# A hybrid state-space, attention and expert block: a new layout of the state-space powers, a shorter phase doubling, a moved norm, and four diagonals on another engine

## Chip, cores and metric

The kernel runs on one core of one Trainium2 chip. The metric is the device time of one execution in microseconds, taken as the median of several runs. The engines are named as the profile names them: PE (TensorE, matmuls; PEld its weight loads), DVE (VectorE), ACT (ScalarE), POOL (GpSimd), and SP, whose queue starts most DMA transfers.

## The reference

The input is 512 tokens of width 1024 in fp32, a memory of 256 tokens, and stream positions. One layer computes, cut to what matters here:

```python
h = rms(x); z = h @ w_in                 # columns: u_ssm 512, c_q 768, c_kv 256, k_rope 32
# (A) state-space: 32 groups of 16 channels, 64 complex states each
a_bar = exp(lam * dt); b_bar = ((a_bar - 1) / lam) * b
states = scan(s_t = a_bar * s_{t-1} + b_bar @ u_t); y = Re(c @ states) + d * u
y = gelu(y); y_ssm = y * sigmoid(y @ w_glu + b_glu)
# (B) latent attention, 8 heads
q = rms(c_q, q_norm_g) @ w_q_up; kv = rms(c_kv, kv_norm_g) @ w_kv_up; rotary; chunk mask
x = x + concat(rms(y_ssm), rms(y_mla)) @ w_out
x = x + cross_attention(rms(x), rms(mem, norm_mem_g))     # 4 heads, 256 memory tokens
x = x + experts(rms(x))                                   # top-1 of 4 groups, top-2 of 8 experts
return rms(x)
```

## The kernel before, in words

Dense weights are used in two parts, a high part `hi` rounded to a shorter float and the rest `lo`, and each product is three matmuls (`mm3`, lines 264 to 269: hi x hi, hi x lo, lo x hi). `next_w` (189) delivers the next weight tile: SP loads `raw`, ACT makes `hi` (204) and DVE subtracts to get `lo` (214). Three `raw`, three `hi` and three `lo` buffers rotate. Activations are split in the same way by `split` (271 to 278), the high part on ACT and the low part on DVE.

The order of the work in the front of the program:
- The input is transposed and split without its norm; the square sums give the row factor `rx` (416), POOL's `pow` being used for the root (`rstd`, 315). `rx_row` (421) spreads `rx` over columns: four diagonal matrices `dg` are multiplied with ones on PE into `pRX`, and ACT copies that to `RX` (427).
- `s5_params` (463) prepares the state-space part on 128 partitions: powers 0 to 8 of `a_bar` as `are` and `aim` (501 to 517), laid out as [power, group], and the matrices `bs`, `bw`, `cx`, `cy`.
- The first projection makes `u_ssm` (741 to 750; `zq` is scaled with `RX` on DVE), then the keys' and values' latents `pkv` (795 to 803), then the queries' latents `pcq` in six parts (860 to 872). `pz`, `pkv`, `pcq` and `pq` share four PSUM banks in turn; the latents `pkv` are read out by ACT (811) and by DVE's `rope` (789 to 792), and the first `pcq` takes the bank of the first `pkv`.
- The queries' norm follows (874 to 879): a column sum on PE, DVE's copy `sc` (355), POOL's `second_rstd`, and two small DVE products `crq`, `srq`.
- The memory is normed and transposed by `norm_T` (331 to 345, called at 889): for each of two tiles a square sum on ACT (329), scale and root on POOL (317, 318), scaling on ACT (338); then for each of eight column blocks two transposes on PE into one of two PSUM banks and a split into `mT` on ACT and DVE.
- The queries are formed (`pq`, 898 to 912), and the memory's values (`pxv`, 955 to 972).

The state-space part runs beside these. A plan by steps (102, 751 to 764) says after which weight tile each piece is put in: `s5_phase` (577) at step 3, and for each quarter q of the groups `s5_a` (619), `s5_b` (656), `s5_d` (686), `s5_e` (722). A piece is queued behind the last weight or matmul instructions issued by then (`aside`, 174). `s5_a` builds `G` (635 to 637) and `V` (648 to 650) on DVE; the operand `vk` of `V` takes the eight powers as innermost index:

```python
def vk(a):
    return a[:, 1:9, gs].rearrange("p k g -> p g k")[:, :, None, :].to_broadcast([128, 8, 16, 8])
```

`s5_phase` squares a unit phase eight times, renormalising each time, with eight DVE operations per level on 16 elements (591 to 598), and then builds the table `tb` by doubling (606 to 613).

After this front come the attention, the output projection, the cross-attention and the experts. The experts' weights (`gu`, `dn`) are loaded by SP into the buffers that the stages before set free (217 on), and the order on each engine is otherwise set by a list with priorities when the program is built.

Of the kernel before, what the change touches and what calls it, by code (L numbers as in the profile page):

```python
# [15 lines left out]
AF = mybir.ActivationFunctionType  # L16
OP = mybir.AluOpType
# [4 lines left out]
NT = 4  # L22
# [82 lines left out]
def build(tc, I, out, dbg=None, stop=None):  # L105
    nc = tc.nc
# [132 lines left out]
    for i in range(8):  # L239
# [4 lines left out]
        n, k = divmod(i, 4)  # L244
# [53 lines left out]
    ident = C.tile([128, 128], F32, name="ident")  # L298
# [29 lines left out]

        return nc.scalar.activation(spare, src, AF.Square, accum_out=acc)

    def norm_T(tiles, name, n_tok, dst, spare, srcs=None):

        st = C.tile([128, 2, 4], F32, name=f"st_{name}")
        for t, a in enumerate(tiles):
          with hp_(HN):
            square_sum(st[:, 0, t:t + 1], a, spare(t))
            rstd(st[:, 1, t:t + 1], st[:, 0, t:t + 1], 1, D)
            nc.scalar.activation(srcs[t] if srcs else a, a, AF.Copy, scale=st[:, 1, t:t + 1])
        src = srcs or tiles
        for k in range(8):  # L340
            ps = bankt(f"pT_{name}{k}")
            for t in range(len(tiles)):
                nc.tensor.transpose(ps[:, t * 128:(t + 1) * 128], src[t][:, k * 128:(k + 1) * 128], ident)
            hi, lo = dst(k)
            split(hi, lo, ps[:, :n_tok], gain(name, k))
# [38 lines left out]
    rx, rx2 = x_st[:, 1], x_st[:, 2]  # L384
    w0 = next_w("ssm")
    rx, rx2 = x_st[:, 1], x_st[:, 2]
# [34 lines left out]
    def rx_row():  # L421
        ps = bankt("pRX")
        for t in range(NT):
            dg = M.tile([128, 128], F32, name=f"dg{t}", tag="sq")
            nc.gpsimd.tensor_scalar(dg, ident, rx[:, t:t + 1], 1.0, OP.mult, OP.mult)
            nc.tensor.matmul(ps[:, t * 128:t * 128 + 128], ones1.to_broadcast([128, 128]), dg, start=True, stop=True)
        nc.scalar.activation(RX, ps, AF.Copy)

# [34 lines left out]
    def s5_params():  # L463
# [3 lines left out]
        def t(name, shape, dt=F32, tag=""):  # L467
            p[name] = SP.tile(shape, dt, name=f"s5_{name}", tag=tag or f"s5_{name}")
            return p[name]
# [37 lines left out]
        for n in (1, 2, 4):  # L507
# [8 lines left out]
            v.tensor_tensor(aim[:, o], are[:, i], bi, OP.mult)  # L516
            v.tensor_tensor(aim[:, o], aim[:, o], t1, OP.add)

        am, den, fre, fim, t0 = (t(n, [128, 32]) for n in ("am", "den", "fre", "fim", "t0"))
        v.tensor_scalar(am, are[:, 7], -1.0, None, OP.add)  # L520
        v.tensor_tensor(den, lre, lre, OP.mult)
# [55 lines left out]
    def s5_phase(p):  # L577
        v = nc.vector

        def t(name, shape, dt=F32, tag=""):  # L580
            return SP.tile(shape, dt, name=f"s5_{name}", tag=tag or f"s5_{name}")

        ph = p["ph"]

        t2 = t("t2", [128, 4, 16])
        pw = t("pw", [128, 6, 2, 16])
        cur = ph
        for lvl in range(-2, 6):
            nx = pw[:, lvl] if lvl >= 0 else t(f"ph{lvl}", [128, 2, 16])
            c0, s0 = cur[:, 0], cur[:, 1]  # L590
            v.tensor_tensor(t2[:, 0], c0, c0, OP.mult)
            v.tensor_tensor(t2[:, 1], s0, s0, OP.mult)
            v.tensor_tensor(t2[:, 2], t2[:, 0], t2[:, 1], OP.add)  # L593
            v.tensor_scalar(t2[:, 2], t2[:, 2], -1.0, 2.0, OP.mult, OP.add)
            v.tensor_tensor(t2[:, 0], t2[:, 0], t2[:, 1], OP.subtract)
            v.scalar_tensor_tensor(t2[:, 3], c0, 2.0, s0, OP.mult, OP.mult)
            v.tensor_tensor(nx[:, 0], t2[:, 0], t2[:, 2], OP.mult)
            v.tensor_tensor(nx[:, 1], t2[:, 3], t2[:, 2], OP.mult)
            cur = nx

        tb = p["tb"] = u("KV", [128, 2, 16, 64], F32, "s5tb")
        tt = t("tt", [128, 2, 16, 32], tag="s5gt")
        nc.gpsimd.memset(tb[:, 0, :, 0:1], 1.0)
        nc.gpsimd.memset(tb[:, 1, :, 0:1], 0.0)
        pl_ = nc.gpsimd if TP else v
        for lvl in range(6):
            n = 1 << lvl
            c_, s_ = (pw[:, lvl, a, None, :, None].to_broadcast([128, 2, 16, n]) for a in range(2))
            o = tb[:, :, :, n:2 * n]
            pl_.tensor_tensor(tt[:, :, :, 0:n], tb[:, :, :, 0:n], s_, OP.mult)  # L610
            pl_.tensor_tensor(o, tb[:, :, :, 0:n], c_, OP.mult)
            pl_.tensor_tensor(o[:, 0], o[:, 0], tt[:, 1, :, 0:n], OP.subtract)
            pl_.tensor_tensor(o[:, 1], o[:, 1], tt[:, 0, :, 0:n], OP.add)
# [5 lines left out]
    def s5_a(p, q):  # L619

        gs = slice(8 * q, 8 * q + 8)
        v = nc.vector
        pg_ = nc.gpsimd if GP & 1 else v
        ph_ = nc.gpsimd if GP & 2 else v

        g_ = SP.tile([128, 8, 9, 16], F32, name=f"s5G{q}", tag="s5G", bufs=2)
        gt = SP.tile([128, 8, 9, 16], F32, name=f"s5gt{q}", tag="s5gt")

        def ck(a):
            return a[:, :, gs].rearrange("p k g -> p g k")[:, :, :, None].to_broadcast([128, 8, 9, 16])  # L630

        def cm(a):
            return a[:, gs, None, :].to_broadcast([128, 8, 9, 16])

        pg_.tensor_tensor(g_, ck(p["are"]), cm(p["cx"]), OP.mult)
        pg_.tensor_tensor(gt, ck(p["aim"]), cm(p["cy"]), OP.mult)
        pg_.tensor_tensor(g_, g_, gt, OP.add)

        vs = SP.tile([128, 8, 16, 8], F32, name=f"s5vs{q}", tag="s5vs")
        vt = SP.tile([128, 8, 16, 8], F32, name=f"s5vt{q}", tag="s5gt")  # L640

        def vk(a):
            return a[:, 1:9, gs].rearrange("p k g -> p g k")[:, :, None, :].to_broadcast([128, 8, 16, 8])

        def vm(a):
            return a[:, gs, 0:16, None].to_broadcast([128, 8, 16, 8])

        ph_.tensor_tensor(vs, vk(p["are"]), vm(p["bs"]), OP.mult)
        ph_.tensor_tensor(vt, vk(p["aim"]), vm(p["bw"]), OP.mult)
        ph_.tensor_tensor(vs, vs, vt, OP.add)  # L650
        rc = SP.tile([128, 4, 64], F32, name=f"s5rc{q}", tag="s5rc", bufs=2)
        nc.scalar.activation(rc, p["rp"][:, 4 * q:4 * q + 4, None].to_broadcast([128, 4, 64]), AF.Copy)
        nc.gpsimd.memset(rc[:, :, 0:1], 0.0)
        return dict(G=g_, vs=vs, rc=rc)
# [216 lines left out]
            nc.vector.tensor_tensor(sqa, sqa, sq, OP.add)  # L871
        step()
    rq = C.tile([128, NT], F32, name="rq")
    colsum_rstd(rq, sqa, 768, "q", True)
    nc.gpsimd.tensor_scalar(rq, rq, 96.0 ** -0.5, 1.0, OP.mult, OP.mult)
    crq, srq = C.tile([128, NT, 16], F32, name="crq"), C.tile([128, NT, 16], F32, name="srq")
    rqb = rq[:, :, None].to_broadcast([128, NT, 16])
    nc.vector.tensor_tensor(crq, cos, rqb, OP.mult)
    nc.vector.tensor_tensor(srq, sin, rqb, OP.mult)

    mT = [u("H", [128, 4, 2, 256], F32R, f"mT{i}") for i in range(2)]

# [3 lines left out]
    def mv(k, c0=0, c1=256):  # L886
        return mT[k // 4][:, k % 4, 0, c0:c1], mT[k // 4][:, k % 4, 1, c0:c1]

    norm_T([mm_t[:, t] for t in range(2)], "norm_mem_g", 256, m_dst,
           lambda t: mT[0][:, 2 * t:2 * t + 2].rearrange("p k a t -> p (k a t)"))  # L890


    Q = [u("H", [128, 2, 8, 100], F32, f"Q{i}") for i in range(2)]
# [1085 lines left out]
```

## Time and profile before

| | |
|---|---|
| median of 3 runs | 732.78 us (732.72 to 732.96) |
| the profiled execution | 733.54 us |
| its span, first to last instruction | 731.4 us |
| busy: PE, DVE, ACT, POOL | 682.5 us, 416.3 us, 248.7 us, 113.8 us |
| mean granted clock of PE | 0.978 |
| DMA moved | 165.84 MB |

The span is what the trace shows; the profiled execution's own time is 2.1 us longer, and 0.76 us longer than the median. A busy share over the whole span averages stages that are limited by different things, so the views below are cut to stretches. In a wait, the engine and line behind the arrow are what came last by the trace. The granted clock is the share of TensorE's full speed.

### The profile page before, as it was taken

What the parts mean: (1) busy time and instruction counts of PE and PEld (TensorE: products, weight loads), DVE (VectorE), ACT (ScalarE), POOL (GpSimd) and SP (SyncE); (2) the same over time, 40 slices, a digit from 0 to 9 for tenths busy, and PEclk for the clock granted to TensorE, in tenths of its full rate; (3) what the DMA queues carried; (4) which work ended last, traced back from release to release, by engine and by line L of the source; (5) the groups of instructions that cost most, each with busy time, mean ns of one, the idle gap of its engine ahead of it and who ended that gap; (6) DMA issues with size and microseconds to landing.
All of it is one profiled execution on the core that took longest, in us unless ns stands there. A gap on an engine that the chain in (4) does not pass through costs nothing.

```text
span 731.4 us, 10262 instructions
## 1 busy us (share of the span) xinstructions
PE 682.5 (93%) x3684; PEld 469.9 (64%) x3684; DVE 416.3 (57%) x975; ACT 248.7 (34%) x511; POOL 113.8 (16%) x172
## 2 busy tenths in 40 slices
PE   5998988987999999999999999999998999998875
PEld 4696877975878887888878788963333333433333
DVE  4799997957477887555466543552533421221127
ACT  5642354344565766334345422221101000000023
POOL 6300002003300001102000001212332232232100
PEclk9999999999999999999999999999999999999996
DMA  7773132435452254232328896869999999999983
GB/s 213 168 206 109 38 74 67 114 123 127 145 164 68 92 153 131 99 84 84 107 80 339 271 338 240 282 251 390 409 408 408 410 404 410 407 413 388 397 337 121
DMA packets 102013, 165.84 MB, mean 227 GB/s; under 512 B 32762, under 2 KB 64606, under 8 KB 98120
## 3 DMA queue, kind: packets, MB, share of 16 engines
q1 hardware_dynamic: 95512, 157.58, 61.0%
q0 software_dynamic: 6432, 7.58, 3.1%
q8 instruction: 30, 0.49, 0.3%
q14 instruction: 23, 0.19, 0.1%
q10 hardware_dynamic: 16, 0.00, 0.0%
HBM read 154.59 MB, written 25.69 MB: 246 GB/s over the span
## 4 chain that ended last, share of the span: by engine, by line
PE 52%; DMA 28%; DVE 13%; ACT 2%; issue 2%; SPq 1%; POOL 0%; DVEq 0%; ACTq 0%
DMA gu<-moe_w_up 15%; DMA dn<-moe_w_down 6%; PE pG L1784 3%; DVE lo L214 2%; PE po L1034 2%; DMA raw<-w_in 2%; PE pX L1443 2%; PE pxq L268 2%; PE pxq L266 2%; PE pxq L267 2%; DMA gu<-moe_w_gate 2%; PE pD L1841 2%; PE pxo L266 2%; PE pPT L1023 2%; PE pxo L267 2%
## 5 line engine op out<-in xcount | busy, mean ns | idle before, releaser
L1784 PE MATMUL pG<-gu,XT 128*64 128x512 f32 x512 | 126.7, 595 | 5.3 <-DMA gu<-moe_w_up 5.2
L214 DVE TENSOR_TENSOR lo<-raw,hi 128x1024 fp32r<-128x1024 f32 (+3 forms) x64 | 75.9, 1190 | 60.5 <-ACT hi L204 60.1
L204 ACT ACTIVATE hi<-raw 128x1024 fp32r<-128x1024 f32 (+3 forms) x64 | 63.9, 1002 | 102.0 <-issue 21.1
L1784 PEld LDWEIGHTS pG<-gu,XT 128*64 128x64 f32 x512 | 40.4, 136 | 71.8 <-issue 68.5
L1841 PE MATMUL pD<-dn,aT 128*64 128x512 f32 x256 | 73.2, 601 | 1.8 <-DMA dn<-moe_w_down 1.8
L1807 DVE SCALAR_TENSOR_TENSOR a<-pG,RS,sl 128x256 f32<-128x256 f32 x16 | 10.7, 670 | 105.8 <-ACT sl L1801 65.4
L1801 ACT ACTIVATE sl<-pG,RS 128x256 f32<-128x256 f32 x16 | 7.6, 474 | 131.9 <-PE pG L1784 131.9
L1841 PEld LDWEIGHTS pD<-dn,aT 128*64 128x64 f32 x256 | 20.5, 136 | 36.4 <-issue 31.6
L1417 DVE TENSOR_TENSOR XT<-pX,gmo 128x512 f32<-128x512 f32 x32 | 22.0, 686 | 20.9 <-PE pX L1768 16.8
L1803 POOL TENSOR_SCALAR YY<-XG,F 128x1024 f32<-128x1024 f32 x13 | 15.2, 1169 | 107.1 <-issue 46.9
L1768 PEld LDWEIGHTS pX<-ident,XG 128*128 128x128 f32 x120 | 15.7, 194 | 25.0 <-issue 17.2
L1849 DVE SCALAR_TENSOR_TENSOR YY<-pD,GT,YY 128x512 f32<-128x512 f32 x26 | 19.5, 749 | 21.1 <-PE pD L1841 21.0
L1827 ACT ACTIVATE aT<-pA 128x256 f32<-128x256 f32 x16 | 6.1, 384 | 61.4 <-PE pD L1841 46.0
L1768 PE MATMUL pX<-ident,XG 128*128 128x128 f32 x120 | 21.0, 298 | 5.3 <-DMA XG<-hd,IX 5.2
L267 PE MATMUL pxq<-gT,hi 128*128 128x512 f32 x64 | 25.6, 400 | 0.0
L266 PE MATMUL pxq<-gT,hi 128*128 128x512 f32 x64 | 25.5, 399 | 0.0
L268 PE MATMUL pxq<-gT,lo 128*128 128x512 f32 x64 | 25.4, 396 | 0.0
L266 PE MATMUL pcq<-hT,hi 128*128 128x512 f32 x48 | 20.0, 416 | 2.8 <-DVE s_t L593 2.8
L267 PE MATMUL pq<-lo,cq 128*128 128x384 f32 x48 | 18.1, 376 | 2.3 <-DVE lo L214 2.3
L268 PE MATMUL pcq<-hT,lo 128*128 128x512 f32 x48 | 19.7, 410 | 0.0
L267 PE MATMUL pcq<-hT,hi 128*128 128x512 f32 x48 | 19.5, 407 | 0.0
L1855 POOL DMA_INDIRECT xd<-YY,IY x14 | 14.7, 1047 | 30.7 <-DVE YY L1849 25.7
(617 smaller groups left out, 1690.0 us busy)
## 6 DMA issues: line engine op xcount, KB each, us to landing
gu<-moe_w_gate SPq DMA_DIRECT2D x64, 512.0 KB
gu<-moe_w_up SPq DMA_DIRECT2D x64, 512.0 KB
dn<-moe_w_down SPq DMA_DIRECT2D x30, 1024.0 KB
raw<-w_in SPq DMA_DIRECT2D x9, 512.0 KB
raw<-xattn_w_v SPq DMA_DIRECT2D x8, 512.0 KB
raw<-xattn_w_k SPq DMA_DIRECT2D x8, 512.0 KB
raw<-w_out SPq DMA_DIRECT2D x8, 512.0 KB
raw<-xattn_w_q SPq DMA_DIRECT2D x8, 512.0 KB
```

Of the source, the lines that this page charges most:

```text
L204: anchor["act"] = nc.scalar.activation(hi, r, AF.Copy)
L214: anchor["dve"] = nc.vector.tensor_tensor(lo, r, hi.bitcast(F32), OP.subtract)
L266: i = nc.tensor.matmul(o, lh, rh, start=start, stop=False)
L267: nc.tensor.matmul(o, lh, rl, start=False, stop=False)
L268: anchor["pe"] = nc.tensor.matmul(o, ll, rh, start=False, stop=stop)
L1417: return v.tensor_tensor(xt, ps.rearrange("p (k t) -> p k t", k=4), gmo[:, 4 * c:4 * c + 4, None].to_broadcast([128, 4, 128]), OP.mult)
L1768: i = nc.tensor.transpose(ps[:, k * 128:k * 128 + 128], xg[:, 4 * c + k], ident)
L1784: i = nc.tensor.matmul(pg[64 * s:64 * s + 64], xt[c][:, kk, 64 * s:64 * s + 64], ew[2 * n + s, c][:, :, kk], start=k == 0, stop=k == 7)
L1803: nc.gpsimd.tensor_scalar(result(n), XG[n % 2], F1[:, n:n + 1], 1.0, OP.mult, OP.mult)
L1841: i = nc.tensor.matmul(pd[64 * s:64 * s + 64], at_[:, f, 64 * s:64 * s + 64], ew[2 * n + s, 2][:, f, c * 512:c * 512 + 512], start=f == 0, ...
L1849: yield v.scalar_tensor_tensor(o, pd, GT[:, n:n + 1], o, OP.mult, OP.add)
L1855: nc.gpsimd.indirect_dma_start(out=o, out_offset=bass.IndirectOffsetOnAxis(ap=IY[:, w, n:n + 1], axis=0), in_=Y, in_offset=None, bounds_ch ...
```

## The change

Four edits:
- In `s5_params` two ACT copies write `ake`, the powers 1 to 8 of `are` and `aim` as [group, power]. In `s5_a` the operand `vk` reads `ake`, whose eight powers lie side by side.
- In `s5_phase` a level has five DVE operations: both squares in one, the renormalising factor with its sign turned, the difference and the double product with their signs turned, and one product of both with the factor.
- `norm_T` takes a function `mid`, called between its norms and its transposes. The queries' norm becomes that function for the memory, so it is issued behind the memory's norms and ahead of its transposes.
- The four diagonals `dg` are made by ACT (a copy with a scale) and not by POOL.

```diff
--- before.py
+++ after.py
@@ -328,7 +328,7 @@
 
         return nc.scalar.activation(spare, src, AF.Square, accum_out=acc)
 
-    def norm_T(tiles, name, n_tok, dst, spare, srcs=None):
+    def norm_T(tiles, name, n_tok, dst, spare, srcs=None, mid=None):
 
         st = C.tile([128, 2, 4], F32, name=f"st_{name}")
         for t, a in enumerate(tiles):
@@ -337,6 +337,8 @@
             rstd(st[:, 1, t:t + 1], st[:, 0, t:t + 1], 1, D)
             nc.scalar.activation(srcs[t] if srcs else a, a, AF.Copy, scale=st[:, 1, t:t + 1])
         src = srcs or tiles
+        if mid is not None:
+            mid()
         for k in range(8):
             ps = bankt(f"pT_{name}{k}")
             for t in range(len(tiles)):
@@ -422,7 +424,7 @@
         ps = bankt("pRX")
         for t in range(NT):
             dg = M.tile([128, 128], F32, name=f"dg{t}", tag="sq")
-            nc.gpsimd.tensor_scalar(dg, ident, rx[:, t:t + 1], 1.0, OP.mult, OP.mult)
+            nc.scalar.activation(dg, ident, AF.Copy, scale=rx[:, t:t + 1])
             nc.tensor.matmul(ps[:, t * 128:t * 128 + 128], ones1.to_broadcast([128, 128]), dg, start=True, stop=True)
         nc.scalar.activation(RX, ps, AF.Copy)
 
@@ -516,6 +518,10 @@
             v.tensor_tensor(aim[:, o], are[:, i], bi, OP.mult)
             v.tensor_tensor(aim[:, o], aim[:, o], t1, OP.add)
 
+        ake = t("ake", [128, 2, 32, 8])
+        for i, a in enumerate((are, aim)):
+            nc.scalar.activation(ake[:, i], a[:, 1:9].rearrange("p k g -> p g k"), AF.Copy)
+
         am, den, fre, fim, t0 = (t(n, [128, 32]) for n in ("am", "den", "fre", "fim", "t0"))
         v.tensor_scalar(am, are[:, 7], -1.0, None, OP.add)
         v.tensor_tensor(den, lre, lre, OP.mult)
@@ -582,20 +588,17 @@
 
         ph = p["ph"]
 
-        t2 = t("t2", [128, 4, 16])
+        t2 = t("t2", [128, 5, 16])
         pw = t("pw", [128, 6, 2, 16])
         cur = ph
         for lvl in range(-2, 6):
             nx = pw[:, lvl] if lvl >= 0 else t(f"ph{lvl}", [128, 2, 16])
-            c0, s0 = cur[:, 0], cur[:, 1]
-            v.tensor_tensor(t2[:, 0], c0, c0, OP.mult)
-            v.tensor_tensor(t2[:, 1], s0, s0, OP.mult)
-            v.tensor_tensor(t2[:, 2], t2[:, 0], t2[:, 1], OP.add)
-            v.tensor_scalar(t2[:, 2], t2[:, 2], -1.0, 2.0, OP.mult, OP.add)
-            v.tensor_tensor(t2[:, 0], t2[:, 0], t2[:, 1], OP.subtract)
-            v.scalar_tensor_tensor(t2[:, 3], c0, 2.0, s0, OP.mult, OP.mult)
-            v.tensor_tensor(nx[:, 0], t2[:, 0], t2[:, 2], OP.mult)
-            v.tensor_tensor(nx[:, 1], t2[:, 3], t2[:, 2], OP.mult)
+
+            v.tensor_tensor(t2[:, 0:2], cur, cur, OP.mult)
+            v.scalar_tensor_tensor(t2[:, 4], t2[:, 0], -2.0, t2[:, 1], OP.add, OP.add)
+            v.tensor_tensor(t2[:, 2], t2[:, 1], t2[:, 0], OP.subtract)
+            v.scalar_tensor_tensor(t2[:, 3], cur[:, 0], -2.0, cur[:, 1], OP.mult, OP.mult)
+            v.tensor_tensor(nx, t2[:, 2:4], t2[:, 4:5].to_broadcast([128, 2, 16]), OP.mult)
             cur = nx
 
         tb = p["tb"] = u("KV", [128, 2, 16, 64], F32, "s5tb")
@@ -639,14 +642,14 @@
         vs = SP.tile([128, 8, 16, 8], F32, name=f"s5vs{q}", tag="s5vs")
         vt = SP.tile([128, 8, 16, 8], F32, name=f"s5vt{q}", tag="s5gt")
 
-        def vk(a):
-            return a[:, 1:9, gs].rearrange("p k g -> p g k")[:, :, None, :].to_broadcast([128, 8, 16, 8])
+        def vk(i):
+            return p["ake"][:, i, gs, None, :].to_broadcast([128, 8, 16, 8])
 
         def vm(a):
             return a[:, gs, 0:16, None].to_broadcast([128, 8, 16, 8])
 
-        ph_.tensor_tensor(vs, vk(p["are"]), vm(p["bs"]), OP.mult)
-        ph_.tensor_tensor(vt, vk(p["aim"]), vm(p["bw"]), OP.mult)
+        ph_.tensor_tensor(vs, vk(0), vm(p["bs"]), OP.mult)
+        ph_.tensor_tensor(vt, vk(1), vm(p["bw"]), OP.mult)
         ph_.tensor_tensor(vs, vs, vt, OP.add)
         rc = SP.tile([128, 4, 64], F32, name=f"s5rc{q}", tag="s5rc", bufs=2)
         nc.scalar.activation(rc, p["rp"][:, 4 * q:4 * q + 4, None].to_broadcast([128, 4, 64]), AF.Copy)
@@ -871,12 +874,14 @@
             nc.vector.tensor_tensor(sqa, sqa, sq, OP.add)
         step()
     rq = C.tile([128, NT], F32, name="rq")
-    colsum_rstd(rq, sqa, 768, "q", True)
-    nc.gpsimd.tensor_scalar(rq, rq, 96.0 ** -0.5, 1.0, OP.mult, OP.mult)
     crq, srq = C.tile([128, NT, 16], F32, name="crq"), C.tile([128, NT, 16], F32, name="srq")
-    rqb = rq[:, :, None].to_broadcast([128, NT, 16])
-    nc.vector.tensor_tensor(crq, cos, rqb, OP.mult)
-    nc.vector.tensor_tensor(srq, sin, rqb, OP.mult)
+
+    def q_norm():
+        colsum_rstd(rq, sqa, 768, "q", True)
+        nc.gpsimd.tensor_scalar(rq, rq, 96.0 ** -0.5, 1.0, OP.mult, OP.mult)
+        rqb = rq[:, :, None].to_broadcast([128, NT, 16])
+        nc.vector.tensor_tensor(crq, cos, rqb, OP.mult)
+        nc.vector.tensor_tensor(srq, sin, rqb, OP.mult)
 
     mT = [u("H", [128, 4, 2, 256], F32R, f"mT{i}") for i in range(2)]
 
@@ -887,7 +892,7 @@
         return mT[k // 4][:, k % 4, 0, c0:c1], mT[k // 4][:, k % 4, 1, c0:c1]
 
     norm_T([mm_t[:, t] for t in range(2)], "norm_mem_g", 256, m_dst,
-           lambda t: mT[0][:, 2 * t:2 * t + 2].rearrange("p k a t -> p (k a t)"))
+           lambda t: mT[0][:, 2 * t:2 * t + 2].rearrange("p k a t -> p (k a t)"), mid=q_norm)
 
 
     Q = [u("H", [128, 2, 8, 100], F32, f"Q{i}") for i in range(2)]
```

## Rows read from the trace of the kernel before

**Rows 1.** The page: busy tenths of the span in 40 equal slices, by engine.

```profile
PE   5998988987999999999999999999998999998875
...
DVE  4799997957477887555466543552533421221127
```

**Rows 2.** Windows: start:end, length, busy time (instructions) by engine, granted clock, DMA, GB/s.

```profile
30.00:156.00 126.00, 115.60 (x715) 99.20 (x714) 115.50 (x282) 52.00 (x96) 6.10 (x26) 0.95 0.40 113
200.00:400.00 200.00, 198.39 (x1158) 162.27 (x1157) 132.78 (x270) 105.39 (x219) 9.11 (x19) 0.99 0.39 124
530.00:700.00 170.00, 157.74 (x709) 60.23 (x708) 47.62 (x105) 10.44 (x27) 47.36 (x46) 1.00 1.01 401
```

**Rows 3.** Waits of PE, 20 to 200 us: total us, times, longest.

```profile
PE pxv L267 <- DVE lo L214: 3.3, 2, 2.1
PE pcq L266 <- DVE s_t L593: 2.8, 1, 2.8
PE pq L267 <- DVE lo L214: 2.3, 1, 2.3
PE pT_norm_mem_g L343 <- ACT mem L338: 2.2, 1, 2.2
...
PE pRX L426 <- POOL dg L425: 1.7, 1, 1.7
```

**Rows 4.** Windows, as Rows 2, right behind the waits at 54.8 and 103 us.

```profile
57.50:60.30 2.80, 2.71 (x7) 2.17 (x8) 2.80 (x20) 0.00 (x0) 0.00 (x0) 0.50 0.60 168
106.00:108.00 2.00, 2.00 (x8) 2.00 (x7) 2.00 (x3) 0.60 (x1) 0.00 (x0) 0.50 0.34 74
```

**Rows 5.** Lines on DVE, 30 to 156 us: count, busy, mean ns, idle before.

```profile
L648 DVE TENSOR_TENSOR s5vs<-s_are,s_bs 128x1024 f32<-128x1024 f32 x4 | 8.2, 2044 | 0.6 <-PE s5vT L680 0.6
L649 DVE TENSOR_TENSOR s5vt<-s_aim,s_bw 128x1024 f32<-128x1024 f32 x4 | 8.0, 2009 | 0.0
...
L635 DVE TENSOR_TENSOR s5G<-s_are,s_cx 128x1152 f32<-128x1152 f32 x4 | 5.4, 1354 | 0.0
...
L650 DVE TENSOR_TENSOR s5vs<-s5vs,s5vt 128x1024 f32<-128x1024 f32 x4 | 5.0, 1238 | 0.0
...
L277 DVE SCALAR_TENSOR_TENSOR mT<-pT_norm_mem_g,G,mT 128x256 fp32r<-128x256 f32 x8 | 3.7, 481 | 3.4 <-ACT mT L276 3.3
```

**Rows 6.** Timeline of DVE around 55 us: start, us, engine, line, tiles.

```profile
53.88 0.20 DVE L591 TENSOR_TENSOR s_t<-s_ph 128x16 f32<-128x16 f32 x1
...
54.83 0.17 DVE L592 TENSOR_TENSOR s_t<-s_ph-2_757 128x16 f32<-128x16 f32 x1
...
56.02 1.22 DVE L214 TENSOR_TENSOR lo<-raw,hi 128x1024 fp32r<-128x1024 f32 x1
...
57.26 0.18 DVE L790 TENSOR_TENSOR rp1k<-pkv,srx 128x32 f32<-128x32 f32 x1
```

**Rows 7.** Timeline of DVE around 103 us.

```profile
100.71 2.01 DVE L648 TENSOR_TENSOR s5vs<-s_are,s_bs 128x1024 f32<-128x1024 f32 x1 [0.62 <-PE s5vT L680]
...
104.47 0.95 DVE L214 TENSOR_TENSOR lo<-raw,hi 128x768 fp32r<-128x768 f32 x1
```

**Rows 8.** Timeline of ACT and POOL: the memory's square sum, then POOL's queue.

```profile
100.28 1.06 ACT L329 ACTIVATE mT<-mem 128x1024 fp32r<-128x1024 f32 x1
...
114.41 0.64 POOL L435 TENSOR_TENSOR rv<-sc,st_x 128x4 f32<-128x4 f32 x1 [28.22 <-DVE sc L355]
...
116.92 1.24 POOL L318 TENSOR_TENSOR st_norm_mem_g<-rv,mhalf 128x1 f32<-128x1 f32 x2
```

**Rows 9.** Timeline of DVE at 151 us.

```profile
151.09 2.35 DVE L214 TENSOR_TENSOR lo<-raw,hi 128x1024 fp32r<-128x1024 f32 x2
```

**Rows 10.** Timeline of POOL and ACT: diagonals, and small ACT operations.

```profile
26.20 0.76 POOL L425 TENSOR_SCALAR dg<-ident,st_x 128x128 f32<-128x128 f32 x2
...
34.06 0.24 ACT L455 ACTIVATE sin<-sck_rope 128x64 f32<-128x64 f32 x1
...
34.36 0.40 ACT L652 ACTIVATE s5rc<-s_rp 128x256 f32<-128x256 f32 x1
```

## The prediction, made before the change was timed

> **What bounds the kernel now.** I read first the page's tenths [rows 1]: PE is full in most slices, and DVE is at 9 in several slices between 20 and 160 us and falls off behind them. Second, the windows [rows 2]. From 30 to 156 us, the stage of all four edits but one, PE is busy 115.6 of 126 us and DVE 115.5, so two engines in strict order share one stage at 92% each. From 200 to 400 us PE is busy 99%, and from 530 to 700 us the DMA queues are full (1.01) and feed the experts' weights. None of the edits touches these two stretches. The weights' loads start as buffers of the dense stages come free, so an earlier front moves PE's stretch and the DMA's stretch forward together. I count a gain in the front one to one.
>
> Third, PE's waits up to 200 us [rows 3]. Four single waits of over 2 us lie in the DVE stage: 2.8 (start of the query latents, `pcq`), 2.3 (`pq`, for a weight's low half), 2.2 (the memory's transposes, for ACT's scaling) and 2.1 (`pxv`, for a low half). That is 9.4 us. One of 1.7 for the diagonals lies ahead of them. [...] At full clock the same cycles take some 0.05 x 126 = 6.3 us less.
>
> **The change part by part.**
>
> *The multiplies of V (L648, L649).* Eight instructions of 1024 elements take 2.04 and 2.01 us on average, 16.2 us together [rows 5]. L650, as large and with all operands in a row, takes 1.24. The old operand steps 32 elements from one power to the next; the new one has the eight powers side by side. L635 also reads a repeated operand and yet takes 1.35 us for 1152 elements, the rate of L650, so repetition alone is not what costs. I take 1.24 us and save 8 x 0.79 = 6.3 us of DVE. The bounds are 1.24, where nothing of the stride is left, and 2.04, where it wasn't the stride. [...]
>
> *Two copies on ACT (`ake`).* 256 elements each; the nearest row is `s5rc`, 128x256 in 0.40 us [rows 10], so 0.8 us. ACT is busy 52 of 126 us [rows 2]. The copies go ahead of the small copies that DVE's `bb` waits for; I charge 0.3 us, between 0 and 0.8.
>
> *Phase doubling.* Eight levels lose three operations each. One level alone takes 0.95 us from start to start (53.88 to 54.83) [rows 6], 0.12 per operation of eight. Five operations, of which three follow each other at about 0.17 to 0.20, give 0.6. Where other work fills the gaps only the issue slot of some 0.09 us is saved (53.88 to 56.02 holds 19 operations and their gaps in 2.14 us). I take 24 x 0.09 = 2.2 us on DVE. The bounds are 8 x 0.1 = 0.8 (all five operations one after another at 0.17, 0.85 instead of 0.95) and 8 x 0.5 = 4.0 (five slots of 0.09 and no gap).
>
> *Diagonals on ACT.* POOL makes two in 0.76 us [rows 10]. On ACT, between 0.24 for 64 elements and 0.40 for 256 [rows 10], one of 128 elements should take some 0.29, and ACT need not stand behind POOL's square of `rx`. The gain on the way to `RX` is 0.4 us, with bounds 1.0 (all four POOL operations against all four of ACT, and no step of POOL before) and a loss of 1.1, one large ACT operation like the 1.06 us one [rows 8] put ahead of them.
>
> *Memory norm ahead of the queries' norm.* No work is added. The second half of the memory's square sum runs on ACT at 100.28, but POOL's queue holds the queries' norm in front, which starts at 114.41 when DVE delivers its sum, and so the memory's root comes at 116.92 [rows 8]. Now POOL can go at 101.4: at most 1.9 us for scale and root (0.64 and 1.24 [rows 8]), then two scalings of about 1.1 us on ACT (the size of the 1.06 row) end near 105.5, some 11 us before the root stands today. The whole wait of 2.2 goes. Moved back in turn is the queries' norm with `crq` and `srq`; its POOL queue is rid of the memory's operations, and the queries' evacuation needs it only when the first `pq` tiles are summed, so I cost it at nothing. Its cover is PE's work on `pq`; with that gone it would cost its chain, from 114.41 to past 118.2 today [rows 8], so 3.8 us or more.
>
> **The sum, two ways.** By waits: (b) `pcq` starts after the read of `pkv` at 57.26 [rows 6], and ahead of that on DVE lie two multiplies (1.6 us) and 19 phase operations, of which 7 go (0.8). 2.4 of the 2.8 go. (c) `pq`: DVE itself waits for PE at 100.71 [rows 7], so nothing saved earlier counts; the two multiplies behind it save 1.6, and the low half at 104.47 comes that much sooner. 1.6 of 2.3 go. (d) 2.2 go. (e) `pxv`: the low halves at 151.09 [rows 9] lie behind the fourth pair, 1.6 of 2.1 go. Together 7.8 us, and if what is left is too short to cost clock, 6.3 more: 14.1 us.
>
> By DVE: 115.5 - 6.3 - 2.2 = 107.0 us of work. If DVE is kept as busy as now (115.5 of 126, 0.917), the stage takes 116.7 us and 9.3 are saved. To save all 14.1, DVE would have to be 96% busy, though it must wait for PE at single buffers (as at 100.71) and PE for it. I take the smaller sum: -9.3 - 0.4 + 0.3 = -9.4 us. What is late next is DVE again, at the queries' sum and at the low halves of `qup`.
>
> The profiled execution took 733.54 us (span 731.4), 0.76 above the median; from it I get 724.1, and against the median of 732.78 it is **723.4 us**.
>
> **The rivals.**
> 1. *All waits and the clock go*: 14.1 and 0.1 from the ends, 718.6 us. For it: each wait by itself is nearly covered. Against it: DVE at 96%.
> 2. *Half-filled waits*: each is cut by half (-4.7), but what is left still costs the clock: 728.1 us. For it: the queues' order is fixed when the program is built, and built anew with other lengths.
> [...]
> 4. *Slower*: the memory's transposes move from a stretch where DVE idles (3.4 us before the eight `mT` splits, 0.48 each [rows 5]) into the full one near 105 us. They share two PSUM banks, so six of them wait in PE's order for a split, each behind one DVE operation of up to 1.35 us [rows 5]: 8.1 us, and the clock's loss stays. Against (b), (c) and (d), 6.2, with (e) not won, that leaves +1.9, 734.7 us. It decides from about five such waits on. Against it: the list puts the splits early, and PE has other matmuls between.
> 5. *No change*: the front is earlier, but a chain behind it (a round trip through DRAM of the state-space part, the weights' stream) keeps its time: 732.8 us. Against it: those loads wait for buffers, and PE is the fuller engine from 200 us on [rows 2].
>
> **How the numbers follow.** Forecast 0.50; rival 1 0.12; rival 2 0.18; rival 3 0.05; rival 4 0.09; rival 5 0.06. Faster by over 0.2% (about 1.5 us, what a measurement of this kernel tells from no change): 0.50 + 0.12 + 0.18 + 0.05 = 0.85; within it 0.06; slower 0.09. The range from 718.0 to 729.5 takes in the forecast and rivals 1 to 3 and leaves out 0.15, and the tails beyond it.
>
> **What would show it.** L648 and L649 near 1.24 us; phase levels at about 0.6; the memory's scaling on ACT near 105 us and no PE wait for it; PE's wait for the read of `pkv` under 1 us; a granted clock above 0.97 over the same work; DVE's busy time there near 107 us. The forecast is wrong if a new PE wait of over 2 us stands before 160 us (at the queries' sum or at `mT`), or if the start of the experts' stage doesn't come earlier by what the front gained.

## The result, and the profile after

The changed kernel takes 725.54 us (median of 4 runs, 724.5 to 725.92) against 732.75 us for the kernel before beside it: ratio 0.990, 95% interval 0.9883 to 0.9917, so 7.2 us faster. The profiled execution took 724.5 us, its span 722.6. Single executions of one kernel lay up to some 7 us apart, so a profile is read for its waits, and the medians for the totals. The two profiled executions here are 9.0 us apart (733.54 and 724.5) and their spans 8.8, where the medians differ by 7.2.

The page of the changed kernel, busy times (its tenths look much as in [rows 1]). DVE's busy time over the whole span was 416.3 us and is 407.2:

```profile
PE 676.0 (94%) x3684; PEld 464.6 (64%) x3684; DVE 407.2 (56%) x951; ACT 251.1 (35%) x517; POOL 115.9 (16%) x168
```

PE's 3684 matmuls were busy for 682.5 us and are busy for 676.0, with a mean granted clock of 0.978 before and 0.990 after. So of the 8.8 us between the two spans 6.5 are matmuls that took less time, and only 2.3 are idle time of PE that went away (48.9 to 46.6). A second trace of the changed kernel (after_again, span 723.8) has 675.9 us of busy time.

Where the 8.8 us between the two traces arise is read best from the start of each stage's first matmul on PE:

| stage | before | after | shift |
|---|---|---|---|
| `pkv` | 41.88 | 40.09 | -1.8 |
| `pcq` | 57.59 | 55.56 | -2.0 |
| `pq` | 102.61 | 98.39 | -4.2 |
| queries' column sum `pc_q` | 113.01 | 107.03 | -6.0 |
| memory's transposes | 118.88 | 107.83 | -11.0 |
| `pxv` | 146.62 | 137.12 | -9.5 |
| next stage (`pckT`) | 173.95 | 168.94 | -5.0 |
| attention (`psc`) | 198.72 | 192.34 | -6.4 |
| experts (`pG`) | 482.63 | 475.07 | -7.6 |

The front runs 9.5 us ahead up to the start of `pxv` and loses 4.5 of it inside that stage; 2.6 come back on the way to the experts, and 1.2 behind their start. The windows of the changed kernel say the same (columns: window, its length, PE, PEld, DVE, ACT, POOL busy with counts, granted clock, DMA share, GB/s). The clock over the front is 0.97 against 0.95 [rows 2], but right behind the wait at `pxv` it is 0.51:

```profile
30.00:156.00 126.00, 114.11 (x738) 98.81 (x737) 107.01 (x240) 54.00 (x95) 8.94 (x24) 0.97 0.42 119
...
144.50:148.00 3.50, 3.46 (x8) 2.81 (x9) 3.43 (x6) 0.00 (x0) 0.00 (x0) 0.51 0.51 150
```

PE's waits of the changed kernel from 20 to 200 us, the answer to [rows 3] (total, times, longest):

```profile
PE pxv L267 <- DVE lo L214: 5.5, 2, 5.2
PE pkv L266 <- DVE zq L752: 2.0, 1, 2.0
PE pxv L266 <- DVE rp1q L793: 1.4, 1, 1.4
...
PE pq L266 <- ACT sq_q L873: 1.2, 1, 1.2
PE pT_norm_mem_g L345 <- DVE mT L277: 0.9, 1, 0.9
...
PE pcq L266 <- DVE rp1k L793: 0.3, 1, 0.3
```

Of the waits of before, 1.7 at `pRX`, 2.5 of 2.8 at `pcq`, the 2.3 at `pq` for a low half and the 2.2 for the memory's scaling are gone. New are 2.0 at `pkv`, 1.2 and 0.7 at `pq`, 0.9 at the memory's transposes and 1.4 at `pxv` for a rotary, and the wait at `pxv` for a low half has grown from 2.1 to 5.2. DVE's lines answer to [rows 5]: the multiplies of `V` took 2044 and 2009 ns and now take as long as the sum behind them:

```profile
L651 DVE TENSOR_TENSOR s5vs<-s_ake,s_bs 128x1024 f32<-128x1024 f32 x4 | 4.9, 1223 | 0.1
L652 DVE TENSOR_TENSOR s5vt<-s_ake,s_bw 128x1024 f32<-128x1024 f32 x4 | 4.9, 1220 | 0.0
L653 DVE TENSOR_TENSOR s5vs<-s5vs,s5vt 128x1024 f32<-128x1024 f32 x4 | 4.9, 1219 | 0.0
```

DVE's timeline of the changed kernel shows three things: `zq` behind other work at 44.65, a phase level in 0.75 us from start to start (51.43 to 52.18), and a low half at 143.28 at the end of a row of small operations:

```profile
42.71 1.36 DVE L639 TENSOR_TENSOR s5gt<-s_aim,s_cy 128x1152 f32<-128x1152 f32 x1
43.98 0.76 DVE L214 TENSOR_TENSOR lo<-raw,hi 128x576 fp32r<-128x576 f32 x1
44.65 1.07 DVE L752 TENSOR_TENSOR zq<-pz,RX 128x512 f32<-128x512 f32 x1
...
51.43 0.19 DVE L597 TENSOR_TENSOR s_t<-s_ph 128x32 f32<-128x32 f32 x1
...
52.18 0.19 DVE L597 TENSOR_TENSOR s_t<-s_ph-2_760 128x32 f32<-128x32 f32 x1
...
100.21 0.75 DVE L277 SCALAR_TENSOR_TENSOR cq<-pcq,G,cq 128x512 fp32r<-128x512 f32 x1 [2.19 <-ACT cq L276]
...
142.67 0.68 DVE L716 TENSOR_TENSOR s5b<-s5s,s5tb 128x512 f32<-128x512 f32 x1
143.28 1.22 DVE L214 TENSOR_TENSOR lo<-raw,hi 128x1024 fp32r<-128x1024 f32 x1
```

On PE, in the same kernel's timeline, `pxv` stands from 139.3 on until that low half comes:

```profile
45.86 0.38 PE L266 MATMUL pkv<-hi,hT 128*128 128x288 f32 x1 [2.03 <-DVE zq L752]
...
138.86 0.47 PE L266 MATMUL pxv<-hi,mT 128*128 128x512 f32 x1 [1.35 <-DVE rp1q L793]
144.54 0.80 PE L267 MATMUL pxv<-lo,mT 128*128 128x512 f32 x1 [5.21 <-DVE lo L214]
```

ACT's timeline: the high half that this low half needs is done at 130.4 (129.35 and 1.05), 13 us before DVE turns to it. At the front, a table load of 1.28 us stands between the two pairs of diagonals (at 24.98 and 27.13) and ahead of `RX`. Further on, the memory's two scalings (L338) stand in front of the copies of the queries' latents, the second behind a wait for POOL:

```profile
25.70 1.28 ACT L457 ACT_TABLE_LOAD   x1
...
28.53 0.60 ACT L429 ACTIVATE RX<-pRX 128x512 f32<-128x512 f32 x1
...
96.07 1.15 ACT L338 ACTIVATE mem<-mem,st_norm_mem_g 128x1024 f32<-128x1024 f32 x1
98.45 1.16 ACT L338 ACTIVATE mem<-mem,st_norm_mem_g 128x1024 f32<-128x1024 f32 x1 [1.23 <-POOL st_norm_mem_g L318]
99.51 0.67 ACT L276 ACTIVATE cq<-pcq,G 128x512 fp32r<-128x512 f32 x1
...
102.11 0.59 ACT L873 ACTIVATE sq_q<-pcq 128x512 f32<-128x512 f32 x1
...
129.35 1.05 ACT L204 ACTIVATE hi<-raw 128x1024 fp32r<-128x1024 f32 x1
```

### The profile page after: what moved, and what is told of

It reads as the page before. It is cut to its first block, busy times and chain, and to the rows that moved or that the text cites. A ratio compares the mean times of both kernels' runs of the same rounds, so it can differ in the third digit from the quotient of the medians.

```text
span 722.6 us, 10249 instructions
## 1 busy us (share of the span) xinstructions
PE 676.0 (94%) x3684; PEld 464.6 (64%) x3684; DVE 407.2 (56%) x951; ACT 251.1 (35%) x517; POOL 115.9 (16%) x168
## 4 chain that ended last, share of the span: by engine, by line
PE 55%; DMA 30%; DVE 6%; ACT 4%; issue 2%; SPq 1%; POOL 1%; DVEq 0%; ACTq 0%
DMA gu<-moe_w_up 18%; DMA dn<-moe_w_down 8%; PE po L1039 2%; PE pX L1448 2%; PE pxq L266 2%; PE pxq L267 2%; PE pxq L268 2%; PE pxo L266 2%; PE pxo L267 2%; DMA raw<-w_in 2%; PE pxo L268 2%; PE pG L1789 2%; PE pcq L266 2%; PE pPT L1028 1%; PE pcq L267 1%
## 5 line engine op out<-in xcount | busy, mean ns | idle before, releaser
L1846 PE MATMUL pD<-dn,aT 128*64 128x512 f32 x256 | 74.9, 616 | 2.0 <-DMA dn<-moe_w_down 2.0
```

The costliest lines, as they stand in the source:

```text
L1846: i = nc.tensor.matmul(pd[64 * s:64 * s + 64], at_[:, f, 64 * s:64 * s + 64], ew[2 * n + s, 2][:, f, c * 512:c * 512 + 512], start=f == 0, ...
```

## The experiments

Each kernel was timed beside the kernel before on the same chip, and the ratio is to that; a ratio is followed by its 95% interval. "..." stands for lines left out of an edit or a view.

**v_fake: the kernel before, with the operand of `V` side by side and nothing else.** `V` multiplies columns of `cx` and `cy` here in place of the powers, so its numbers are others; the instructions and their order on every queue are those of before.

```diff
-            return a[:, 1:9, gs].rearrange("p k g -> p g k")[:, :, None, :].to_broadcast([128, 8, 16, 8])
+            return a[:, gs, None, 0:8].to_broadcast([128, 8, 16, 8])
...
-        ph_.tensor_tensor(vs, vk(p["are"]), vm(p["bs"]), OP.mult)
-        ph_.tensor_tensor(vt, vk(p["aim"]), vm(p["bw"]), OP.mult)
+        ph_.tensor_tensor(vs, vk(p["cx"]), vm(p["bs"]), OP.mult)
+        ph_.tensor_tensor(vt, vk(p["cy"]), vm(p["bw"]), OP.mult)
```

> The kernel before, but the two multiplies of V read a stand-in whose eight values lie side by side (columns of C, so V holds other numbers); every engine's order stays as before, only the eight multiplies should shorten from 2.03 to about 1.23 us. If DVE sets the pace of the front (my theory): the waits for pkv's read, for pq's low half and for pxv's low half each lose about 1.6 us and part of the clock's 6.3 us comes back: 4 to 8 us off, 725 to 729 us. If the gain comes from the new order that the builder makes and not from the durations (rival): 1 us off at most, 731.5 us or more. If the stride was not what cost, L648 and L649 stay at 2.0 us and nothing changes.

Measured: 726.72 us against 732.69, ratio 0.9911 (0.9879 to 0.9943): 6.0 us faster, in the range of the theory. DVE's lines of this kernel, and PE's wait at `pxv` (25 to 160 us):

```profile
L649 DVE TENSOR_TENSOR s5vt<-s_cy,s_bw 128x1024 f32<-128x1024 f32 x4 | 4.9, 1232 | 0.0
L648 DVE TENSOR_TENSOR s5vs<-s_cx,s_bs 128x1024 f32<-128x1024 f32 x4 | 4.9, 1232 | 0.6 <-PE s5vT L680 0.6
```

```profile
PE pxv L267 <- DVE lo L214: 0.9, 1, 0.9
```

The layout alone carries most of the gain; by the intervals this run can't be told from the full change. The operand's repetition is still there, so it was the step of 128 bytes from one power to the next that cost 0.8 us per multiply. In the old order the wait at `pxv` falls from 2.1 to 0.9, nearly as step (e) had it; a wait of 2.1 for the memory's scaling stays. The gain lies elsewhere than in the full change: PE's busy time is 683.4 us here, as before (682.5), and its idle time falls from 48.9 to 41.4.

**v_strided: the changed kernel, with `V` reading the old operand (`ake` is still written).** Order as in the changed kernel on every queue.

```diff
...
-            return p["ake"][:, i, gs, None, :].to_broadcast([128, 8, 16, 8])
+            return a[:, 1:9, gs].rearrange("p k g -> p g k")[:, :, None, :].to_broadcast([128, 8, 16, 8])
...
```

> The changed kernel, with ake still written, but the multiplies of V reading the old strided powers; the order of every engine is that of the changed kernel, so only the eight durations go back to 2.0 us. If DVE sets the pace: 4 to 7 us above the changed kernel, 729.5 to 732.5 us. If the new order carries the gain: within 1.5 us of it, 725.5 to 727 us.

Measured: 734.59 us, ratio 1.0017 (1.0002 to 1.0032). Without the layout the other three edits and their new order gain nothing. The layout is worth 9.0 us here (734.59 against 725.54, timed apart), more than the 4 to 7 expected and than the 6.4 us of DVE's time that it saves (8 x 0.80). One of DVE's lines and PE's waits (25 to 160 us) of this kernel:

```profile
L651 DVE TENSOR_TENSOR s5vs<-s_are,s_bs 128x1024 f32<-128x1024 f32 x4 | 8.1, 2028 | 0.0
```

```profile
PE pxv L267 <- DVE lo L214: 5.2, 1, 5.2
PE pq L266 <- ACT hi L204: 3.9, 1, 3.9
```

The 3.9 us has a cause that the prediction didn't see. POOL's timeline of this kernel, and below it DVE's:

```profile
97.40 5.27 POOL L317 TENSOR_SCALAR rv<-st_norm_mem_g 128x1 f32<-128x1 f32 x1 [14.11 <-ACT mT L329]
102.75 1.60 POOL L318 TENSOR_TENSOR st_norm_mem_g<-rv,mhalf 128x1 f32<-128x1 f32 x1
104.44 0.19 POOL L317 TENSOR_SCALAR rv<-st_norm_mem_g 128x1 f32<-128x1 f32 x1
104.71 0.54 POOL L318 TENSOR_TENSOR st_norm_mem_g<-rv,mhalf 128x1 f32<-128x1 f32 x1
```

```profile
97.44 1.35 DVE L640 TENSOR_TENSOR s5G<-s5G,s5gt 128x1152 f32<-128x1152 f32 x1
98.71 2.06 DVE L651 TENSOR_TENSOR s5vs<-s_are,s_bs 128x1024 f32<-128x1024 f32 x1
100.67 2.00 DVE L652 TENSOR_TENSOR s5vt<-s_aim,s_bw 128x1024 f32<-128x1024 f32 x1
...
107.18 0.75 DVE L277 SCALAR_TENSOR_TENSOR cq<-pcq,G,cq 128x512 fp32r<-128x512 f32 x1 [3.24 <-ACT cq L276]
```

An operation on one element per partition takes POOL 5.27 us and ends at 102.67, when the second multiply ends; its like at 104.44, with DVE idle, takes 0.19. So in the new order the memory's norm on POOL stands until the strided multiplies are through, and ACT's scaling and PE behind it wait; this is read from the rows, and no run isolated it. The 5.2 us at `pxv` stand here too: that wait belongs to the new order, not to `V`.

**mem_only: the kernel before with the memory's norm moved.** The edit is that of the full change, alone.

```diff
+        if mid is not None:
+            mid()
...
-           lambda t: mT[0][:, 2 * t:2 * t + 2].rearrange("p k a t -> p (k a t)"))
+           lambda t: mT[0][:, 2 * t:2 * t + 2].rearrange("p k a t -> p (k a t)"), mid=q_norm)
```

> The kernel before with only the memory's norm put ahead of the queries' norm; DVE's order is unchanged. My theory: the 2.2 us wait for the memory's scaling goes and the slow clock behind it (some 1.5 us): 2 to 4 us off, 729 to 731 us. Rival: on ACT the two scalings now stand ahead of the last copies of the queries' latents and wait there for POOL, so the wait comes back at pq or at the queries' sum: 0 to 1 us off, 731.8 to 733 us.

Measured: 730.0 us (9 runs, 727.6 to 734.8), ratio 0.9958 (0.9939 to 0.9976). The time is the theory's, but the profile shows the rival's waits, and it is that of the slowest of the nine runs (734.79 us), so it can't show where the gain of the others lies. In it PE waits 2.4 us at `pq` for ACT's `sq_q` in place of the 2.2 for the memory, and POOL's timeline is slow at the same place (before, the pairs took 1.11 and 1.24 us):

```profile
102.79 3.02 POOL L317 TENSOR_SCALAR rv<-st_norm_mem_g 128x1 f32<-128x1 f32 x2 [15.32 <-ACT mT L329]
105.89 2.85 POOL L318 TENSOR_TENSOR st_norm_mem_g<-rv,mhalf 128x1 f32<-128x1 f32 x2
```

**phase_only and dg_only: the kernel before with the phase doubling alone, and with the diagonals alone.** The first has the change's edit in `s5_phase`; the second is:

```diff
-            nc.gpsimd.tensor_scalar(dg, ident, rx[:, t:t + 1], 1.0, OP.mult, OP.mult)
+            nc.scalar.activation(dg, ident, AF.Copy, scale=rx[:, t:t + 1])
```

> The kernel before with only the shorter phase doubling. By the sum: 7 of 19 operations go ahead of the read of pkv, 0.8 us, and at most 2.2 us of DVE in all: 0.5 to 2.5 us off, 730 to 732.2 us. Rival: the builder sorts the queues anew, which decides more than the 2.2 us: outside 729.5 to 733 us.

> The kernel before with only the diagonals made by ACT. By the sum: RX some 0.4 us sooner (0 to 1), and DVE, which starts its full stretch with it, passes that on: 0.2 to 1 us off, 731.7 to 732.5 us. Rival: PE is not what waits there, and nothing is passed on: 732.5 to 733 us; or ACT's order puts other work ahead: up to 1 us slower.

Measured: phase_only 732.65 us against 733.22, ratio 0.9997 (0.9976 to 1.0018), no change, though DVE's busy time over the span falls from 416.3 to 412.5. A level takes 0.75 us there too (53.82 to 54.57). That kernel's order on DVE is another as well, and at `pxv` it is the order of the changed kernel: the low half stands behind four rotaries and `s5_d` and starts at 150.75, and PE's wait is

```profile
PE pxv L267 <- DVE lo L214: 5.0, 1, 5.0
```

Up to the start of `pxv` this kernel runs 2.1 us ahead of before (144.48 against 146.62), and at the start of the next stage 3.4 behind (177.36 against 173.95). The wait at this place is 2.1 in dg_only, 1.5 in mem_only and 0.9 in v_fake, so of the four edits it is the shorter phase doubling that brings the order with the late low half.

dg_only 728.06 us (7 runs, 727.37 to 731.68), ratio 0.9937 (0.9917 to 0.9957), 4.6 us by the ratio and outside every range expected. Its profile is of a run of 730.98 us and doesn't show 4.6 us: the experts start at 481.93 us, only 0.7 ahead of before. PE's wait at `pRX` is 0.6 and a wait of 2.4 at `pkv` is new.

**no_mem and no_dg: the changed kernel without the moved norm, and without the moved diagonals.** Each undoes one edit.

> The changed kernel with the queries' norm back ahead of the memory's norm. My theory: the wait of 2.2 us for the memory's scaling is back, with the slow clock behind it: 2 to 4 us slower than the changed kernel. Rival: in the changed kernel the move has only traded that wait for those at pq and pxv: within 1 us of it.

> The changed kernel with the four diagonals back on POOL. By my sum they are worth 0.4 us: 0 to 1 us slower than the changed kernel. Rival, from the run with the diagonals alone (4.6 us off): they are worth more, by letting the sine's table load and RX go earlier and by the order that follows: 3 to 5 us slower.

Measured, beside the changed kernel once more: after_again 725.86 us, 0.9904 (0.9876 to 0.9932); no_mem 725.63, 0.9894 (0.9873 to 0.9915); no_dg 725.43, 0.9894 (0.9871 to 0.9917). All three are the same within their intervals, some 2 us either way. Their waits suggest why, each edit trading one wait for another; first no_mem (25 to 160 us), where the memory's wait is back and the one for `sq_q` gone, then no_dg, where the diagonals' wait is back and the one at `pkv` gone:

```profile
PE pT_norm_mem_g L343 <- ACT mem L338: 2.3, 1, 2.3
```

```profile
PE pRX L428 <- POOL dg L427: 2.3, 1, 2.3
```

> The changed kernel once more, as the mark for the other three runs on the same chip: 0.990 of the kernel before, as measured at first; if that first set was a lucky one, 0.992 or more.

So the gains don't add: by the ratios the four edits alone took off 0.9 (v_fake), 0.4 (mem_only), 0.6 (dg_only) and 0.0 (phase_only) per cent of the time, and all four together 1.0.

**lo_first: the changed kernel, with one DVE instruction moved.** The first low half of `pxv`'s weight is queued ahead of a rotary of the queries (second half of the heads, second tile) instead of behind it and its followers.

```diff
...
+        if i == 19:
+            behind(ropes[1, 1], anchor["dve"])
...
-        nc.vector.tensor_tensor(t0, sv, c[:, None, None, :].to_broadcast(full), OP.mult)
+        first = nc.vector.tensor_tensor(t0, sv, c[:, None, None, :].to_broadcast(full), OP.mult)
...
+        return first
...
-              rope(q[:, :, 64:96], pv[:, :, 64:96], crq[:, t], srq[:, t], 4, f"q{hh}{t}")
+              ropes[hh, t] = rope(q[:, :, 64:96], pv[:, :, 64:96], crq[:, t], srq[:, t], 4, f"q{hh}{t}")
```

> The changed kernel, with one DVE subtraction (the low half of the first weight tile of the memory's values) put ahead of the rotary of the second query tile; the other queues keep their order. In the changed kernel PE waits 5.2 us for it at 139.3 us and then runs at half clock. My theory: the gain of 9.5 us that the trace shows at the start of pxv is given back there, by DVE's new order alone: 3 to 6 us less than the changed kernel, 719.5 to 722.5 us. Rival: the next weight tiles reach ACT late by SP's queue, so the wait comes back one or two tiles later: within 1.5 us of the changed kernel, 724 us or more.

> The run with one DVE subtraction put ahead of the second rotary, beside the changed kernel on one chip. If the place of that subtraction gives back part of the gain: 2 to 4 us less than the changed kernel. Rival: the 2.9 us seen at first were the difference of two chips: within 1 us of it.

Measured: 722.64 us, 0.9853 (0.9819 to 0.9886), and once more as lo_again 722.92 us, 0.9856 (0.9829 to 0.9882). The changed kernel beside lo_again took 725.86, so the one instruction is worth 2.9 us; the two intervals just touch (0.9829 to 0.9882 and 0.9876 to 0.9932), but the first set gives the same 2.9 against 725.54, and every run of that set (721.43 to 723.08) is below the changed kernel's fastest (724.48). It is just short of the 3 to 6 expected at first. PE's timeline of lo_first, and DVE's:

```profile
140.71 0.50 PE L270 MATMUL pxv<-lo,mT 128*128 128x512 f32 x1 [1.99 <-DVE lo L215]
...
146.88 0.50 PE L270 MATMUL pxv<-lo,mT 128*128 128x512 f32 x1 [1.38 <-DVE lo L215]
```

```profile
139.44 1.21 DVE L215 TENSOR_TENSOR lo<-raw,hi 128x1024 fp32r<-128x1024 f32 x1
140.57 0.28 DVE L795 TENSOR_TENSOR rp0q<-pq,crq 128x128 f32<-128x128 f32 x1
...
145.61 1.21 DVE L215 TENSOR_TENSOR lo<-raw,hi 128x1024 fp32r<-128x1024 f32 x1
```

The wait of 5.2 becomes 2.0 and 1.4, because the next low half is late in its turn. By its median this is the fastest kernel of the study, with `scale_late` and `best` about 1 us behind.

**scale_late and best.** scale_late queues the memory's two scalings behind the last square of the queries' latents on ACT; best does this, the edit of lo_first, and queues `zq` ahead of the first `G` multiply.

```diff
-            nc.scalar.activation(srcs[t] if srcs else a, a, AF.Copy, scale=st[:, 1, t:t + 1])
+            i = nc.scalar.activation(srcs[t] if srcs else a, a, AF.Copy, scale=st[:, 1, t:t + 1])
+            if mid is not None:
+                behind(i, last_sq)
...
-            nc.scalar.activation(sq, ps, AF.Square)
+            last_sq = nc.scalar.activation(sq, ps, AF.Square)
```

> The changed kernel with the two scalings of the memory put on ACT behind the last square of the queries' latents. My theory: ACT, standing before the second scaling for POOL's root, holds up the queries' latents; without that PE's wait of 1.2 us at pq goes: 1 to 2.5 us below the changed kernel, 723 to 724.5 us. Rival: the memory's transposes are late then, or the 5.2 us wait at pxv takes the gain up: within 1 us of it, 724.5 to 726.5 us.

> The changed kernel with three instructions put elsewhere: the low half ahead of the second rotary (as in the run of that alone, 2.9 us), the scaling of the output of the fourth state-space projection ahead of the first products of G on DVE (PE waits 2.0 us for it at 43.8 us), and the two scalings of the memory on ACT behind the last square of the queries' latents (PE waits 1.2 us and DVE 2.2 us there). If what is left of the gain is lost at these three places: 4 to 8 us below the changed kernel, 717.5 to 721.5 us. If DVE's work is the floor and waits only move: like the run with the low half alone, 721.5 to 724 us.

Measured beside each other: scale_late 723.44 us, 0.9857 (0.9832 to 0.9881); best 723.75, 0.9855 (0.9828 to 0.9883). In scale_late the wait for `sq_q` is gone and the 5.2 at `pxv` stays. Its interval overlaps that of after_again (from 0.9876) and just misses that of the first set (from 0.9883), and it wasn't timed beside the changed kernel, so a gain of 2 to 3 us is likely and not shown. In best PE still waits 2.2 at `pkv` and 4.8 at `pxv` in two parts: put together, the moves gained nothing more, as the rival had it.

## Why the prediction was right

The time was forecast at 723.4 us, 718.0 to 729.5; measured are 725.54. The sign and the size hold, with 2.2 us less gain than taken. The layout of `V` was rightly seen as the main step. The rest of the sum came out partly by luck: the other edits were to bring a few us more, and what the runs show of them is gains and losses that cancel. And 725.5 lies midway between the forecast and rival 2's 728.1, so the time alone doesn't choose between these two. Point by point:

- **The multiplies of V** were the right step with the right price: 1.22 us for a forecast 1.24, and that it wasn't the stride (the bound of 2.04, and the 0.05 of rival 3) is ruled out by v_fake. DVE's time over the whole span fell by 9.1 us where 8.5 (6.3 and 2.2) were taken. The two copies on ACT took 0.69 and 0.66 us, not 0.40; they read the powers in the old steps of 128 bytes, and no wait of PE shows them.
- **Phase doubling** removed the 24 instructions and brought a level to 0.75 us, not 0.6: where an operation needs the one just before it, the starts lie 0.2 us apart (51.75, 51.95, 52.18). Alone it saves DVE 3.8 us and gives nothing that can be measured, and it brings the new order that (e) meets.
- **(b) and (c) held in their own place**: 2.8 fell to 0.3 at `pcq`, and the 2.3 for the low half at `pq` went, where 1.6 was taken; 1.2 and 0.7 for other producers stand at `pq` now. But a wait of 2.0 at `pkv` took the place of the one at `pcq`, one stage earlier. It is there in every kernel here with the diagonals on ACT, and in none with them on POOL. The **diagonals** were valued at 0.4 on the way to `RX`, and this step failed: ACT starts `RX` at 28.53 us, where it started it at 28.55, because the table load of 1.28 us stands between the diagonals. PE's wait at `pRX` goes all the same, and PE reaches `pkv` 1.8 us sooner, where it then waits for `zq`, which DVE does at 44.65 behind a multiply of `G` and a low half. In the change the diagonals are worth nothing that can be measured (no_dg). The 4.6 us that dg_only shows alone stay unexplained.
- **(d) was mis-sized and its cover overlooked.** The 2.2 went, as forecast. But "at most 1.9 us for scale and root" was 4.8 from the first scale to the last root (93.60 to 98.42), with DVE busy up to 98.01; and 1.9 was too little by its own trace, since the 0.64 is the row of another operation and the memory's two scales took 1.11. The scalings went into ACT's queue ahead of the queries' copies, which the prediction had costed at nothing. PE waits 1.2 and DVE 2.2 there. The net is nothing that can be measured (no_mem).
- **(e) failed.** It was to fall from 2.1 to 0.5 and became 5.2, with the clock at 0.51 for 3.5 us behind it. The prediction reasoned with the old order of DVE and shortened durations. The builder made a new order in which a subtraction that was ready at 130.4 stands behind four rotaries of the queries, the last products of `V` and a quarter's `s5_d` until 143.28, while PE needs it at 139.3. phase_only shows which edit brings this order. This is rival 2's argument ("built anew with other lengths") at one place. lo_first and its repeat put 2.9 us on it; the gain that is missing is 2.2 (9.4 taken, 7.2 measured).
- **The sum** by DVE's share came nearer than the one by waits (14.1), and its reason for the smaller number held: each edit aimed at one wait has moved it to another. But its premise, DVE as busy as before, did not hold. From 30 us to the first matmul of `pckT` DVE was busy 126.66 of 143.95 us (0.88) and is busy 115.18 of 138.94 (0.83), so 11.5 us less work there bought 5.0 us of time. What PE gained it gained more by the clock than by waits: over the whole span 6.5 us of busy time against 2.3 of idle time, and over the stretch just named the clock went from 0.95 to 0.98. That the front's gain goes to the end was right: -7.6 at the experts' start and -8.8 at the end of the same two traces. The forecast's own sign of error, a new PE wait of over 2 us before 160 us, is there at `pxv` and barely at `pkv`. DVE's 107.01 us from 30 to 156 us equals the forecast by chance: this window now holds some work that lay behind it.
- The first rival (all waits and the clock, whose 0.05 is what the 0.95 of [rows 2] lacks to 1.00) is right about much of the clock and wrong about the waits, which mostly moved. That the clock counts in PE's time shows at `pxv` in the changed kernel: its matmuls start 0.43 us apart where 0.50 is granted (145.56 to 147.27) and 0.23 apart where 1.00 is (148.28 to 148.97). The fourth (transposes in a full stretch) came to 0.9 us of waits there, and the fifth fell to the experts' earlier start.

Left open: dg_only's 4.6 us and where mem_only's gain lies, and whether scale_late and lo_first add up without the third move; that pair was not tried. The phase doubling was not undone inside the change, so whether the change would be faster without it isn't known; v_fake, without it, has the shorter wait at `pxv`.

## What to carry to other kernels

Look first at large DVE operations that run slower per element than their neighbours, and lay the operand out so that the innermost index is side by side; that was most of this gain. In this stage, with two engines both at 92%, a wait that was cut came back at the next late producer, and work saved on DVE didn't always show either (3.8 us in phase_only, and no time). So time an edit both alone and inside the whole change before giving it a price. After any edit that changes lengths, compare the order of each engine's queue with the old one: one ready subtraction, done 13 us later, took back 2.9 us.

## What the hardware showed

**An fp32 operand that steps 128 bytes at each element cost DVE two thirds more.** 1024 elements took 2.03 us with one operand in steps of 128 bytes, and 1.22 with it side by side, everything else equal (v_strided and the changed kernel). Only this one step was tried. The products of `G` read the same powers in the same steps, but each one sixteen times in a row, and take 1.35 us for 1152 elements, the rate of the operands side by side; so the step costs where each element takes it. Why it does, no run shows.

**POOL's small operations stretch beside DVE's.** In the changed kernel, POOL's timeline over the memory's norm, with DVE busy nearly without a gap from 92.99 to 98.01:

```profile
93.60 0.79 POOL L317 TENSOR_SCALAR rv<-st_norm_mem_g 128x1 f32<-128x1 f32 x1 [14.03 <-ACT mT L329]
94.47 1.56 POOL L318 TENSOR_TENSOR st_norm_mem_g<-rv,mhalf 128x1 f32<-128x1 f32 x1
96.16 0.64 POOL L317 TENSOR_SCALAR rv<-st_norm_mem_g 128x1 f32<-128x1 f32 x1
96.89 1.53 POOL L318 TENSOR_TENSOR st_norm_mem_g<-rv,mhalf 128x1 f32<-128x1 f32 x1
```

A root takes 1.5 us here and 0.54 where DVE is idle (104.71 in v_strided); a scale takes 0.6 to 0.8 against 0.19, and 5.27 beside the strided multiplies. Spans on POOL are rough in the profile, but three of these scales end within 0.05 us of the end of a DVE operation. The ends of the roots fall on no end on DVE, and no run here isolated a cause. Why POOL stood through three DVE operations in v_strided, and through one in the changed kernel, is not settled.
